# HGRN output norm per half of the columns, and splits of finished blocks queued behind the last late projection's finish

## The chip, the cores and the metric

The kernel runs on one core of a Trainium2 chip. TensorE (PE) multiplies matrices and puts its results into PSUM; VectorE (DVE), ScalarE (ACT) and GpSimd (POOL) do the elementwise work; SyncE (SP) issues most DMAs. Each engine takes its instructions from a queue of its own, in order, and waits there until the semaphores of the one at the head allow it. The metric is the device time of one launch in microseconds (us); less is better.

## The reference

One layer of a hybrid decoder trunk, in float32, on 1024 tokens of 1024 columns. A projection feeds three groups of heads, whose outputs are put side by side and multiplied by `w_out`. The change touches the norm at the end of the first group and the preparation of those outputs for `w_out`.

```python
z = rmsnorm(h, norm_mix_g[l]) @ w_in[l]
a_q, a_f, a_i, a_g, b_q, b_k, b_v, c_in = jnp.split(z, splits, axis=-1)
o_a = hgrn2_mix(a_q, a_f, a_i, a_g, lbs[l], hgrn_gnorm_g[l])
o_b = dilated_window_mix(b_q, b_k, b_v)
o_c, v_first = rwkv7_mix(c_in, ...)
h = h + jnp.concatenate([o_a, o_b, o_c], axis=-1) @ w_out[l]
...
# in hgrn2_mix, 4 heads of 128 columns, chunks of 64 tokens:
#   S_t = diag(f_t) S_(t-1) + (1 - f_t) i_t^T,  o_t = S_t^T q_t
o = o * lax.rsqrt(jnp.mean(o * o, axis=-1, keepdims=True) + NORM_EPS)
o = o.reshape(B_, S_, HG_WIDTH) * gnorm_g * jax.nn.silu(g_raw)
```

A gated MLP with a short convolution, an embedding gate and a last norm follow; they are not changed.

## The kernel before

**Products.** Each float32 operand is split into a high part, rounded to a type that PE multiplies quickly (`xh`, `whi`), and the rest (`xl`, `wlo`). A product is three matmuls: `xh` by `whi` (L137), `xl` by `whi` (L139), `xh` by `wlo` (L141). `split_x` (L157 to 162) makes the two parts of half a block of activations, 128 x 512: a cast on ACT (L160) and a subtraction (L162), on DVE for the first half of the tokens and on POOL for the second.

**The mixed stage.** Between about 440 and 600 us of the span several streams of work are interleaved. They are Python generators; `interleave` steps through them in a fixed order written out in `phase_mix` (with the tables `LATE` and `TURNS`), and the framework's scheduler then settles each engine's order from that by its own estimates. Stream A runs `hgrn_head` for heads 0 and 2, stream B for heads 1 and 3 (`handover` lets the second head of a pair begin before the first has ended). Stream C is the window attention `swa`; F is `project_late`, the projections that are left for this stage, by halves of the tokens; M is filler.

**`hgrn_head`.** For each chunk size the scores `hsc` are taken from `qt` and `ks` (L990), masked into `hS` by a predicated copy on DVE (L992), and `qt` and `hk` are scaled for the next size (L1003, L1001). Values and keys are transposed on PE (`vt`, L1018 and L1024) and copied by ACT (`hV`, L1019; `hkt`, L1025). Running states `hst` are made on DVE one from the other (L1048). The output `ho` has 1024 tokens as 8 blocks of 128, and is made in two halves of 512 columns: four blocks of matmuls into a bank of PSUM (`hpo`, L1058 and L1060) and a copy by ACT (L1061). Then comes the norm, on all 1024 columns: square on ACT (`hsq`, L1065), sums of each block on DVE (`hss`, L1067), mean and epsilon on DVE (L1068), the power -1/2 on POOL (`hrs`, L1070), the multiply on DVE (L1072). PE transposes the result, four blocks for each half (`vt`, L1078), and DVE multiplies by gain and gate (L1079). `o_split` (L1201) splits the finished block for `w_out`.

**The window attention.** PE makes logits `swq` (L1143), DVE masks them into `lg` (L1153), ACT takes the exponential (L1155), PE transposes `lg` (`swt`, L1169), ACT and DVE copy that to `pT` (L1170), PE multiplies by the values (`swo`, L1183), ACT copies to `ob` (L1184).

**PSUM.** `hsc`, `hpo`, `vt`, `swt`, `swo`, `zp` and others take turns in four banks of one pool ("mx"). PE can write a new tile only when the engine that empties the earlier tile of that bank is done.

**`project_late`.** For each left-over block of columns and each half of the tokens, 24 matmuls go into `zp`, and `finish` (L455) scales them (L320, DVE), applies a sigmoid (L460, ACT) and, for gates, multiplies (L462, DVE). The result goes to memory and is read back by the head that needs it. The last block is number 23, the gate of head 3. After it, blocks that were finished before the place for their splits existed (`self.done`: 6, 7, 0, 4, 1) are split by `o_split`, one a step. In the program's text they come behind the last projection; nothing orders them behind its `finish` in the engines' queues.

**The output projection.** `phase_out` multiplies by `w_out` (`dp`), blocks 6, 7, 0, 1, 4, 2, 3, 5 in turn. Its first matmuls fill PE from about 540 us on.

Of the kernel before, what the change touches and what calls it, by code (L numbers as in the profile page):

```python
# [10 lines left out]
F32 = mybir.dt.float32  # L11
F32R = mybir.dt.float32r
U8 = mybir.dt.uint8
AF = mybir.ActivationFunctionType
ALU = mybir.AluOpType
AX = mybir.AxisListType
PSUM = bass.MemoryType.PSUM

P = 128
T = 1024  # L20
HT = 512
# [68 lines left out]
class Trunk:  # L90
# [362 lines left out]
            yield  # L453

    def finish(self, kind, dst, src, r):  # L455
        if kind == 2:
            self.nc.vector.tensor_tensor(dst, src, r, ALU.mult)
        else:
            self.scale(src, r)
            self.nc.scalar.activation(dst, src, AF.Sigmoid)  # L460
        if kind in (1, 3):
            self.nc.vector.tensor_tensor(dst, dst, src, ALU.mult)  # L462

    def project_late(self, js):


        nc = self.nc
        for j in js:
            w = self.load_w(self.a["w_in"][j])
            t = self.keep.tile([P, T], F32, tag="zst", name=self.nm("zst"), bufs=2)  # L470
            d = self.zpool.tile([P, T], F32, tag=f"z{j}", name=f"z{j}")
            kind = (j - 8) % 4 if j < 24 else 2
            turn = j < 24 and kind < 3
            for hf in (0, 1):
                ps = self.mxp.tile([P, HT], F32, tag="mx", name=self.nm("zp"))
                self.dense({hf: ps}, w, self.X, ND, halves=(hf,))
                dst = slice((hf ^ turn) * HT, ((hf ^ turn) + 1) * HT)
                r = self.R[:, hf * HT:(hf + 1) * HT]
                self.finish(kind, t[:, dst], *((ps[:, ::-1], r[:, ::-1]) if turn and hf else (ps, r)))
                nc.sync.dma_start(d[:, dst], t[:, dst])  # L480
                if hf:
                    self.z[j] = d
                yield
        self.O = self.xall()
        for k in self.done:
            self.o_split(k)
            yield

    def zload(self, j, pool_slot, eng=None):
# [439 lines left out]
    def hgrn_head(self, h):  # L929
        nc, mxp, par, spool = self.nc, self.mxp, self.par, self.spool  # L930
        j0 = 8 + 4 * h
# [8 lines left out]
        k = self.slot("hk")  # L940
# [88 lines left out]
        def at(cc, swap=False):  # L1029
            c = (4 + cc if cc < 4 else 7 - cc) ^ (4 if swap else 0)  # L1030
            return slice(c * P, (c + 1) * P)

        for hf in (0, 1):
# [6 lines left out]
            for c in range(4):  # L1040
# [3 lines left out]
                dst = st[:, (cc + 1) * P:(cc + 2) * P]  # L1044
# [7 lines left out]
        o = self.slot("ho")  # L1052
        for hf in (0, 1):
            po = mxp.tile([P, 4, P], F32, tag="mx", name=self.nm("hpo"))
            for c in range(4):
                cc = 7 - c if hf == 0 else c
                s = at(cc)
                nc.tensor.matmul(po[:, c, :], S[:, s], V[:, s], start=True, stop=cc == 0)  # L1058
                if cc:
                    nc.tensor.matmul(po[:, c, :], qt[:, s], st[:, cc * P:(cc + 1) * P], start=False, stop=True)  # L1060
            nc.scalar.copy(o[:, hf * HT:(hf + 1) * HT], po.rearrange("p c v -> p (c v)"))  # L1061
        yield
        oa = self.zload(j0 + 3, self.slot)
        sq = self.slot("hsq")
        nc.scalar.activation(sq, o, AF.Square)  # L1065
        ss = spool.tile([P, 8], F32, tag="hss", name=self.nm("hss"))
        nc.vector.tensor_reduce(ss, sq.rearrange("p (c v) -> p c v", v=P), AX.X, ALU.add)  # L1067
        nc.vector.tensor_scalar(ss, ss, 1.0 / P, EPS, ALU.mult, ALU.add)  # L1068
        rs = spool.tile([P, 8], F32, tag="hrs", name=self.nm("hrs"))
        nc.gpsimd.tensor_tensor(rs, ss, self.mhalf[:, :8], ALU.pow)  # L1070
        o3 = o.rearrange("p (c v) -> p c v", v=P)
        nc.vector.tensor_tensor(o3, o3, rs.unsqueeze(2).broadcast_to([P, 8, P]), ALU.mult)  # L1072
        yield
        for hf in (0, 1):
            sl = slice((1 - hf) * HT, (2 - hf) * HT)
# [739 lines left out]
```

## Time and profile before

| | |
|---|---|
| median of 3 runs | 1427.42 us (1426.49 to 1429.19) |
| the profiled execution's own time | 1426.41 us |
| its span in the profile | 1424.6 us |
| mean granted clock of TensorE | 0.992 |
| four norms (square L1065, four heads) | 4.3 us of ACT |
| four norms (sums L1067 and multiply L1072) | 4.9 and 4.9 us of DVE |

In rows of a timeline the first number is the start in us from the span's start, the second the duration, then engine, line, operation, output <- input, partitions x elements, and how many such instructions stand together. What stands in brackets is the engine's idle time before the row and what ended it. In rows of groups, busy us and mean ns of one stand behind the first bar, idle time before them behind the second. A row of waits gives the waiting engine and line, the engine and line waited for, the us in total, how often, and the longest. A row of windows gives the stretch and its length, then busy us and number of instructions for PE, PE's weight loads, DVE, ACT and POOL, the granted clock of PE, the DMA share and GB/s.

### The profile page before, as it was taken

The page shows a single profiled execution, that of the slowest core. Times are in us where ns is not written, and L with a number is a line of the kernel's source. Part 1 is how long each engine was busy: PE and PEld are TensorE (multiplying, and loading weights), DVE is VectorE, ACT ScalarE, POOL GpSimd, SP SyncE. Part 2 cuts the span into 40 slices and gives each one's busy share as a digit, 9 for nine tenths or more (in the row PEclk, how much of TensorE's full clock was granted, in tenths as well). Part 3 has the DMA queues.
Part 4 walks back from the last instruction along what each step waited for, and adds up shares of the span by engine and source line. Part 5 has one row for each costly group of instructions (what it writes and reads, how often), then busy time and mean ns, then how long its engine had stood idle before and what let it go on. Part 6 is the DMA issues. An engine that isn't in the chain of part 4 may idle for free.

```text
span 1424.6 us, 22342 instructions
## 1 busy us (share of the span) xinstructions
PE 1381.9 (97%) x8642; PEld 1118.0 (78%) x8642; DVE 1066.8 (75%) x1629; ACT 602.5 (42%) x1015; POOL 392.5 (28%) x286
## 2 busy tenths in 40 slices
PE   8989999999999999999999999999999999999996
PEld 6768777777778768787788888888888888888885
DVE  7597363964666796468788888898888799778675
ACT  7411323123155485254544444443434444455542
POOL 5321012210122141221244544454543000002431
PEclk9999999999999999999999999999999999999998
DMA  6124111240432211753332233333324963441443
GB/s 220 45 82 119 61 46 61 81 119 32 154 143 104 84 61 40 262 178 117 119 111 91 94 106 102 106 102 111 112 96 147 356 214 111 126 141 47 135 158 113
DMA packets 80122, 167.61 MB, mean 118 GB/s; under 512 B 19984, under 2 KB 22288, under 8 KB 80016
## 3 DMA queue, kind: packets, MB, share of 16 engines
q1 hardware_dynamic: 66496, 146.52, 30.6%
q10 hardware_dynamic: 12656, 16.52, 3.4%
q0 software_dynamic: 864, 3.15, 0.6%
q8 instruction: 68, 1.11, 0.3%
q14 instruction: 38, 0.31, 0.1%
HBM read 119.76 MB, written 46.40 MB: 117 GB/s over the span
## 4 chain that ended last, share of the span: by engine, by line
PE 48%; issue 3%; DVE 2%; POOL 1%; ACT 1%; DMA 0%; POOLq 0%; ACTq 0%; DVEq 0%
PE bg L1302 16%; PE bv L1302 12%; PE bv L1596 7%; PE bg L1596 7%; PE dp L141 1%; PE dp L137 1%; PE dp L139 1%; POOL wlo L116 1%; PE bv L137 0%; PE bv L139 0%; PE bv L141 0%; DVE h L1692 0%; POOL xh L162 0%; DVE gt L1691 0%; ACT whi L114 0%
## 5 line engine op out<-in xcount | busy, mean ns | idle before, releaser
L137 PE MATMUL dp<-xh,whi 128*128 128x512 f32 x544 | 189.2, 408 | 6.9 <-DVE r L501 2.9
L139 PE MATMUL dp<-xl,whi 128*128 128x512 f32 x544 | 182.7, 396 | 0.8 <-DVE xl L411 0.8
L141 PE MATMUL dp<-xh,wlo 128*128 128x512 f32 x544 | 181.1, 394 | 0.0
L116 POOL TENSOR_TENSOR wlo<-wraw,whi 128x512 fp32r<-128x512 f32 x60 | 81.6, 1360 | 321.4 <-ACT whi L114 257.1
L116 POOL TENSOR_TENSOR wlo<-raw,whi 128x512 fp32r<-128x512 f32 x84 | 134.7, 1622 | 76.0 <-ACT whi L114 76.0
L114 ACT CAST whi<-wraw 128x512 fp32r<-128x512 f32 x120 | 72.8, 617 | 155.7 <-PE dp L139 107.3
L1302 PE MATMUL bg<-t,whi 128*128 128x512 f32 x352 | 133.3, 389 | 0.0
L137 PEld LDWEIGHTS dp<-xh,whi 128*128 128x128 f32 x544 | 99.4, 189 | 34.9 <-issue 6.2
L139 PEld LDWEIGHTS dp<-xl,whi 128*128 128x128 f32 x544 | 102.2, 189 | 23.8 <-DVE xl L411 1.1
L141 PEld LDWEIGHTS dp<-xh,wlo 128*128 128x128 f32 x544 | 102.7, 189 | 22.9 <-issue 0.8
L116 POOL TENSOR_TENSOR wlo<-s,whi 128x512 fp32r<-128x512 f32 x44 | 64.0, 1454 | 175.0 <-ACT whi L114 175.0
L1596 PE MATMUL bg<-t,whi 128*128 128x512 f32 x308 | 95.3, 390 | 0.0
L1596 PE MATMUL bv<-t,whi 128*128 128x512 f32 x308 | 94.8, 389 | 0.0
L114 ACT CAST whi<-raw 128x512 fp32r<-128x512 f32 x88 | 52.6, 619 | 94.3 <-issue 48.3
L114 ACT CAST whi<-s 128x512 fp32r<-128x512 f32 x66 | 38.9, 620 | 121.4 <-PE bg L1302 113.6
L1302 PEld LDWEIGHTS bg<-t,whi 128*128 128x128 f32 x352 | 66.1, 188 | 13.6
L190 POOL TENSOR_TENSOR rst<-rst,mhalf 128x4 f32<-128x4 f32 (+1 forms) x9 | 9.9, 1102 | 235.6 <-DVE rst L186 218.5
L1302 PE MATMUL bg<-t,wlo 128*128 128x512 f32 x176 | 67.2, 389 | 0.0
L1596 PEld LDWEIGHTS bv<-t,whi 128*128 128x128 f32 x308 | 57.9, 188 | 11.9
L1596 PEld LDWEIGHTS bg<-t,whi 128*128 128x128 f32 x308 | 57.8, 188 | 12.0
L1592 ACT CAST t<-t 128x512 fp32r<-128x512 f32 x77 | 47.8, 622 | 45.5 <-PE bv L1596 31.8
L116 DVE TENSOR_TENSOR wlo<-wraw,whi 128x512 fp32r<-128x512 f32 x60 | 49.7, 829 | 20.6 <-ACT whi L114 20.4
(417 smaller groups left out, 3415.1 us busy)
## 6 DMA issues: line engine op xcount, KB each, us to landing
raw<-in_ffn_up_dram SPq DMA_DIRECT2D x44, 512.0 KB, 3.5
wraw<-in_w_in_dram SPq DMA_DIRECT2D x28, 512.0 KB, 3.4
z<-zst SPq DMA_DIRECT2D x18, 512.0 KB, 2.8
gb<-ct SPq DMA_DIRECT2D x33, 256.0 KB, 2.2
t<-gb SPq DMA_DIRECT2D x33, 256.0 KB, 2.7
t<-gt SPq DMA_DIRECT2D x33, 256.0 KB, 2.7
zl<-z SPq DMA_DIRECT2D x16, 512.0 KB, 4.2
wraw<-in_ple_gate_dram SPq DMA_DIRECT2D x16, 512.0 KB, 3.4
```

The source lines that it names most:

```text
L114: self.cast = nc.scalar.copy(hi, src).ins
L116: eng.tensor_tensor(lo, src, hi.bitcast(F32), ALU.subtract)
L137: nc.tensor.matmul(ps[hf], wh, xh[hf], start=first, stop=False)
L139: nc.tensor.matmul(ps[hf], wh, xl[hf], start=False, stop=False)
L141: nc.tensor.matmul(ps[hf], wl, xh[hf], start=False, stop=last)
L190: nc.gpsimd.tensor_tensor(r2, r, self.mhalf[:, :n], ALU.pow)
L1302: nc.tensor.matmul(ps, w[part == 2][:, s], X[k][part == 1], start=start and k == part == 0, stop=k == 3 and part == 2, skip_group_check=no ...
L1592: nc.scalar.copy(xh, x)
L1596: nc.tensor.matmul(ps[m], wt[part == 2][:, m * P:(m + 1) * P], (xh, xl)[part == 1], start=k == part == 0, stop=k == NK - 1 and part == 2)
```

## The change

`finish` returns the instructions that end it. `project_late` keeps those of its last call, the second half of block 23 (a sigmoid on ACT and a multiply on DVE), and issues each of the five waiting `o_split` behind them (`issue_after`): 10 casts on ACT, 5 subtractions on DVE and 5 on POOL. This sets an order in the queues; it adds no data dependence and no DMA.

In `hgrn_head` square and sums are taken per half, each right behind the copy of that half; the gate's load and the tiles of the norm are taken before the first copy; the multiply is written as two of 512 columns. Mean and power stay as they were, one instruction each for both halves. No matmul is added or taken away.

```diff
--- before.py
+++ after.py
@@ -453,13 +453,15 @@
             yield
 
     def finish(self, kind, dst, src, r):
+        ends = []
         if kind == 2:
-            self.nc.vector.tensor_tensor(dst, src, r, ALU.mult)
+            ends.append(self.nc.vector.tensor_tensor(dst, src, r, ALU.mult))
         else:
             self.scale(src, r)
-            self.nc.scalar.activation(dst, src, AF.Sigmoid)
+            ends.append(self.nc.scalar.activation(dst, src, AF.Sigmoid))
         if kind in (1, 3):
-            self.nc.vector.tensor_tensor(dst, dst, src, ALU.mult)
+            ends.append(self.nc.vector.tensor_tensor(dst, dst, src, ALU.mult))
+        return ends
 
     def project_late(self, js):
 
@@ -476,14 +478,17 @@
                 self.dense({hf: ps}, w, self.X, ND, halves=(hf,))
                 dst = slice((hf ^ turn) * HT, ((hf ^ turn) + 1) * HT)
                 r = self.R[:, hf * HT:(hf + 1) * HT]
-                self.finish(kind, t[:, dst], *((ps[:, ::-1], r[:, ::-1]) if turn and hf else (ps, r)))
+                ends = self.finish(kind, t[:, dst], *((ps[:, ::-1], r[:, ::-1]) if turn and hf else (ps, r)))
                 nc.sync.dma_start(d[:, dst], t[:, dst])
                 if hf:
                     self.z[j] = d
                 yield
         self.O = self.xall()
         for k in self.done:
-            self.o_split(k)
+            with ExitStack() as order:
+                for i in ends:
+                    order.enter_context(self.tc.issue_after(i.ins))
+                self.o_split(k)
             yield
 
     def zload(self, j, pool_slot, eng=None):
@@ -1058,18 +1063,21 @@
                 nc.tensor.matmul(po[:, c, :], S[:, s], V[:, s], start=True, stop=cc == 0)
                 if cc:
                     nc.tensor.matmul(po[:, c, :], qt[:, s], st[:, cc * P:(cc + 1) * P], start=False, stop=True)
-            nc.scalar.copy(o[:, hf * HT:(hf + 1) * HT], po.rearrange("p c v -> p (c v)"))
-        yield
-        oa = self.zload(j0 + 3, self.slot)
-        sq = self.slot("hsq")
-        nc.scalar.activation(sq, o, AF.Square)
-        ss = spool.tile([P, 8], F32, tag="hss", name=self.nm("hss"))
-        nc.vector.tensor_reduce(ss, sq.rearrange("p (c v) -> p c v", v=P), AX.X, ALU.add)
+            s = slice(hf * HT, (hf + 1) * HT)
+            if hf == 0:
+                oa = self.zload(j0 + 3, self.slot)
+                sq = self.slot("hsq")
+                ss = spool.tile([P, 8], F32, tag="hss", name=self.nm("hss"))
+            nc.scalar.copy(o[:, s], po.rearrange("p c v -> p (c v)"))
+            nc.scalar.activation(sq[:, s], o[:, s], AF.Square)
+            nc.vector.tensor_reduce(ss[:, 4 * hf:4 * hf + 4], sq[:, s].rearrange("p (c v) -> p c v", v=P), AX.X, ALU.add)
+        yield
         nc.vector.tensor_scalar(ss, ss, 1.0 / P, EPS, ALU.mult, ALU.add)
         rs = spool.tile([P, 8], F32, tag="hrs", name=self.nm("hrs"))
         nc.gpsimd.tensor_tensor(rs, ss, self.mhalf[:, :8], ALU.pow)
         o3 = o.rearrange("p (c v) -> p c v", v=P)
-        nc.vector.tensor_tensor(o3, o3, rs.unsqueeze(2).broadcast_to([P, 8, P]), ALU.mult)
+        for c in (slice(0, 4), slice(4, 8)):
+            nc.vector.tensor_tensor(o3[:, c], o3[:, c], rs[:, c].unsqueeze(2).broadcast_to([P, 4, P]), ALU.mult)
         yield
         for hf in (0, 1):
             sl = slice((1 - hf) * HT, (2 - hf) * HT)
```

The first place is DVE's queue at the norm of head 0, beside a `pT` copy of the window attention (`hss` sums, `ho` output, `hrs` power; `hS` and `qt` are another head's masked scores and queries). Before:

```order
L1067 TENSOR_REDUCE hss_745_4528<-hsq_744_4526 128x8
L1170 COPY pT_734_4494<-swt_736_4501 128x384
L1170 COPY pT_737_4506<-swt_739_4513 128x384
L1068 TENSOR_SCALAR hss_745_4528<-hss_745_4528 128x8
L992 COPY_PREDICATED hS_683_4210<-cmask_77,hsc_747_4534 128x4x64
L1072 TENSOR_TENSOR ho_724_4433<-ho_724_4433,hrs_746_4531 128x1024
L1003 TENSOR_TENSOR qt_671_4148<-qt_671_4148,hT_684_4212 128x2x32x8
```

After the change:

```order
L1073 TENSOR_REDUCE hss_728_4446<-hsq_727_4445 128x4
L997 COPY_PREDICATED hS_683_4210<-cmask_77,hsc_730_4461 128x4x64
L1008 TENSOR_TENSOR qt_671_4148<-qt_671_4148,hT_684_4212 128x2x64x4
L1073 TENSOR_REDUCE hss_728_4446<-hsq_727_4445 128x4
L1075 TENSOR_SCALAR hss_728_4446<-hss_728_4446 128x8
L1080 TENSOR_TENSOR ho_724_4433<-ho_724_4433,hrs_746_4533 128x512
L1178 COPY pT_737_4502<-swt_739_4509 128x384
L1178 COPY pT_740_4514<-swt_742_4521 128x384
L1080 TENSOR_TENSOR ho_724_4433<-ho_724_4433,hrs_746_4533 128x512
L997 COPY_PREDICATED hS_683_4210<-cmask_77,hsc_747_4537 128x4x64
L1008 TENSOR_TENSOR qt_671_4148<-qt_671_4148,hT_684_4212 128x2x32x8
```

The sums stand in two rows, the scaling (now L1075) and the first half of the multiply have moved ahead of both `pT` copies, and the second half stands behind them.

The second place is ACT's queue at the end of the last late projection, from the casts ahead of the sigmoid on (`whi` is a cast of weights). Before:

```order
L160 CAST xh_885_5252<-zl_827_4970 128x512
L114 CAST whi_1017_5897<-wraw_1015_5895 128x512
L160 CAST xh_891_5258<-ob_635_3976 128x512
L160 CAST xh_895_5262<-oc_295_1813 128x512
L114 CAST whi_1020_5901<-wraw_1015_5895 128x512
L160 CAST xh_897_5264<-oc_546_3441 128x512
L460 ACT_TABLE_LOAD
L460 ACTIVATE zst_838_4990<-zp_874_5180 128x512
L1019 COPY hV_875_5209<-vt_876_5210 128x512
L1019 COPY hV_875_5209<-vt_877_5216 128x512
L1025 COPY hkt_878_5222<-vt_879_5223 128x512
L1025 COPY hkt_878_5222<-vt_880_5229 128x512
```

After the change:

```order
L114 CAST whi_1020_5913<-wraw_1015_5907 128x512
L461 ACT_TABLE_LOAD
L461 ACTIVATE zst_838_4996<-zp_874_5186 128x512
L1024 COPY hV_875_5215<-vt_876_5216 128x512
L1024 COPY hV_875_5215<-vt_877_5222 128x512
L160 CAST xh_911_5284<-oc_295_1813 128x512
L160 CAST xh_895_5268<-oc_295_1813 128x512
L160 CAST xh_913_5286<-oc_546_3441 128x512
L1030 COPY hkt_878_5228<-vt_879_5229 128x512
L1030 COPY hkt_878_5228<-vt_880_5235 128x512
L160 CAST xh_897_5270<-oc_546_3441 128x512
L1192 COPY ob_822_4951<-swo_919_5304 128x128
```

The casts `xh` have left the place ahead of the sigmoid; three of them stand between the `hV` and the `hkt` copies now and others further down, between the copies of the window attention.

The third place is DVE's queue at the norm of head 2. Before:

```order
L1067 TENSOR_REDUCE hss_950_5464<-hsq_949_5462 128x8
L992 COPY_PREDICATED hS_870_5156<-cmask_77,hsc_952_5470 128x4x64
L1068 TENSOR_SCALAR hss_950_5464<-hss_950_5464 128x8
L1003 TENSOR_TENSOR qt_855_5086<-qt_855_5086,hT_871_5158 128x2x32x8
L1072 TENSOR_TENSOR ho_943_5421<-ho_943_5421,hrs_951_5467 128x1024
L1170 COPY pT_959_5515<-swt_961_5522 128x384
L1170 COPY pT_962_5527<-swt_964_5534 128x384
```

After the change:

```order
L1073 TENSOR_REDUCE hss_947_5440<-hsq_946_5439 128x4
L997 COPY_PREDICATED hS_870_5162<-cmask_77,hsc_949_5455 128x4x64
L1008 TENSOR_TENSOR qt_855_5092<-qt_855_5092,hT_871_5164 128x2x64x4
L1073 TENSOR_REDUCE hss_947_5440<-hsq_946_5439 128x4
L1013 TENSOR_TENSOR hT_871_5164<-hT_871_5164 128x16
L162 TENSOR_TENSOR xl_910_5283<-ob_822_4951,xh_909_5282 128x512
L1075 TENSOR_SCALAR hss_947_5440<-hss_947_5440 128x8
L997 COPY_PREDICATED hS_870_5162<-cmask_77,hsc_952_5479 128x4x64
L1080 TENSOR_TENSOR ho_943_5427<-ho_943_5427,hrs_951_5475 128x512 x2
L1008 TENSOR_TENSOR qt_855_5092<-qt_855_5092,hT_871_5164 128x2x32x8
L1178 COPY pT_959_5524<-swt_961_5531 128x384
L1178 COPY pT_962_5536<-swt_964_5543 128x384
```

A moved subtraction (`xl_910`) stands between the second sum and the scaling, and both halves of the multiply and a `qt` stand ahead of the `pT` copies.

On PE, at the norm of head 3, the transposes `vt` of the normed output stand among matmuls of the output projection. Before:

```order
L139 MATMUL dp_1014_5846<-xl_904_5271,whi_1002_5828 128x512
L139 MATMUL dp_1014_5846<-xl_888_5255,whi_1002_5828 128x512
L141 MATMUL dp_1014_5846<-xh_903_5270,wlo_1003_5830 128x512
L141 MATMUL dp_1014_5846<-xh_887_5254,wlo_1003_5830 128x512
L137 MATMUL dp_1022_5910<-xh_911_5278,whi_1012_5842 128x512
L1078 MATMUL vt_998_5758<-cst_76,ho_991_5728 128x128 x4
L1078 MATMUL vt_999_5764<-cst_76,ho_991_5728 128x128 x4
L137 MATMUL dp_1022_5910<-xh_895_5262,whi_1012_5842 128x512
```

After the change:

```order
L139 MATMUL dp_1014_5858<-xl_904_5277,whi_1002_5840 128x512
L139 MATMUL dp_1014_5858<-xl_888_5261,whi_1002_5840 128x512
L1086 MATMUL vt_998_5770<-cst_76,ho_991_5737 128x128 x4
L1086 MATMUL vt_999_5776<-cst_76,ho_991_5737 128x128 x4
L141 MATMUL dp_1014_5858<-xh_903_5276,wlo_1003_5842 128x512
L141 MATMUL dp_1014_5858<-xh_887_5260,wlo_1003_5842 128x512
L137 MATMUL dp_1022_5922<-xh_911_5284,whi_1012_5854 128x512
L137 MATMUL dp_1022_5922<-xh_895_5268,whi_1012_5854 128x512
```

The eight transposes stand three output matmuls earlier.

## The prediction

> **What bounds the kernel now.** I read the views in this order: the page's busy times, for the engine that sets the time; the table of windows, for the stretch in which the changed instructions run; PE's waits in that stretch, as the most that can be won there; then the timeline around each wait.
>
> ```profile
> span 1424.6 us, 22342 instructions
> ...
> PE 1381.9 (97%) x8642; PEld 1118.0 (78%) x8642; DVE 1066.8 (75%) x1629; ACT 602.5 (42%) x1015; POOL 392.5 (28%) x286
> ```
> ```profile
> 440.00:600.00 160.00, 152.45 (x1368) 123.59 (x1365) 113.61 (x226) 82.15 (x160) 44.83 (x36) 1.00 0.33 116
> 580.00:620.00 40.00, 40.00 (x178) 33.14 (x177) 17.24 (x25) 12.29 (x21) 9.16 (x7) 1.00 0.63 224
> ```
> ```profile
> PE vt L1078 <- DVE ho L1072: 3.0, 2, 1.8
> PE vt L1024 <- ACT hV L1019: 2.4, 1, 2.4
> PE hsc L990 <- DVE qt L1003: 1.0, 2, 0.6
> PE zp L137 <- DVE pT L1170: 0.5, 1, 0.5
> PE swt L1169 <- DVE hS L992: 0.2, 1, 0.2
> PE zp L137 <- ACT hV L1019: 0.2, 1, 0.2
> ```
>
> TensorE (PE) is busy 97% of the span, and the change takes no matmul away. Every changed instruction runs between 440 and 600 us, where PE is idle for 160.00 - 152.45 = 7.55 us at full granted clock (the 1.00 behind POOL's column). The six waits make 7.3 of that. So 7.3 us, 0.51% of the time, is the most that the change can win. It can lose more, because VectorE (DVE) has 113.61 busy us of these 160 and stands in most of those rows. From 580 on PE has no idle time at all. A shift of PE's work at 575 thus reaches the end one for one, and the sum below is a sum of PE's waits.
>
> **The prices.** The norm is now done on 512 columns.
>
> ```profile
> L215 ACT ACTIVATE sqt<-h 128x512 f32<-128x512 f32 x41 | 25.6, 631 | 46.4 <-DVE h L1692 20.7 <-DVE h L1232 15.9 <-DVE acc L216 3.9
> L1065 ACT ACTIVATE hsq<-ho 128x1024 f32<-128x1024 f32 x4 | 4.3, 1068 | 0.1
> L1067 DVE TENSOR_REDUCE hss<-hsq 128x8 f32<-128x1024 f32 x4 | 4.9, 1218 | 5.1 <-ACT hsq L1065 5.1
> L1072 DVE TENSOR_TENSOR ho<-ho,hrs 128x1024 f32<-128x1024 f32 x4 | 4.9, 1226 | 6.2 <-POOL hrs L1070 6.2
> ```
>
> A half square costs 0.63 us (the 128x512 square of L215), so two cost 0.19 more than one whole. No row shows a half reduce or half multiply. Each lies between half of the whole, 0.61, and the whole, 1.22. I take 0.61, since the square at half size comes near half. Twenty-four such halves replace twelve wholes, and ACT and DVE have 49% and 29% of the stretch idle, so their added work costs PE something only where it stands ahead of something that PE waits for. The small scaling (TENSOR_SCALAR) and the power on POOL still take both halves at once. A tile's power therefore starts after its second reduce, 0.63 - 1.07 + 0.61 - 1.22 = about 1.05 us sooner at best, and the first half of the multiply ends 0.61 sooner again.
>
> [...]
>
> **Head 0 (456 to 465 us).**
>
> ```profile
> 456.50 1.05 ACT L1065 ACTIVATE hsq<-ho 128x1024 f32<-128x1024 f32 x1
> ...
> 456.67 1.27 POOL L1001 TENSOR_TENSOR hk<-hk,hT 128x512 f32<-128x512 f32 x1 [5.62 <-ACT ks L977]
> ...
> 458.72 1.01 DVE L1170 COPY pT<-swt 128x384 f32<-128x384 f32 x2
> ...
> 459.36 1.71 PE L1183 MATMUL swo<-pT,sV 128*64 128x128 f32 x28
> ...
> 459.89 1.67 POOL L1070 TENSOR_TENSOR hrs<-hss,mhalf 128x8 f32<-128x8 f32 x1 [1.96 <-DVE hss L1068]
> ...
> 463.56 0.69 PE L990 MATMUL hsc<-qt,ks 128*64 128x64 f32 x16 [0.59 <-DVE qt L1003]
> ...
> 464.80 0.50 PE L137 MATMUL zp<-xh,whi 128*128 128x512 f32 x1 [0.55 <-DVE pT L1170]
> ```
>
> Before, DVE made its two pT copies at 458.72, ahead of the scaling and the multiply, and PE entered swo at 459.36, whose bank of PSUM the first copy empties. Now the scaling and the first half multiply stand ahead of both copies. Second half square 456.50 to 457.13; half reduce to 457.8; POOL free of hk at 457.94; the power until about 459.6; half multiply until 460.3; the first copy (half of 1.01) until 460.8. PE waits 460.8 - 459.36 = 1.4. That delay swallows the later waits of 0.59 and 0.55, for qt and pT, which DVE reaches before PE now. Net 1.4 - 1.14 = **+0.3**. Bounds: -1.1, if the copies are hardly late; +0.6 with a power of 2.01 (its longest, below).
>
> **Head 1 (500 to 507 us).**
>
> ```profile
> 500.04 2.01 POOL L1070 TENSOR_TENSOR hrs<-hss,mhalf 128x8 f32<-128x8 f32 x1 [6.42 <-DVE hss L1068]
> ...
> 504.55 0.69 DVE L320 TENSOR_TENSOR zp<-zp,rstd 128x512 f32<-128x512 f32 x1
> ...
> 505.64 0.55 PE L1169 MATMUL swt<-cst,lg 128*128 128x128 f32 x3 [0.16 <-DVE hS L992]
> ```
>
> Nothing on PE waited for this multiply. After it, the scaling of the projection's first half, which was done at 504.55, now stands behind the hk, zl and qt rows of head 2, some 2 us later, and the mask copy and qt for the second-last scores behind that. I work out 0.45 us of wait for that qt in place of the 0.16. **+0.3**, bounds -0.2 (the wait goes) and +1.2 (the 2 us less 0.8, which four window matmuls that now run ahead fill: half of the eight's 1.56 in the next view).
>
> **The late projection's end (519 to 540 us).** This is the moved split. Ten ACT casts, five DVE and five POOL subtractions now stand behind the finish's sigmoid and multiply; no DMA and no matmul are issued by them.
>
> ```profile
> 519.33 1.77 DVE L162 TENSOR_TENSOR xl<-zl,xh 128x512 fp32r<-128x512 f32 x1
> ...
> 520.50 1.72 POOL L162 TENSOR_TENSOR xl<-ob,xh 128x512 fp32r<-128x512 f32 x1
> ...
> 520.56 1.56 PE L1143 MATMUL swq<-zl,zl 64*128 64x512 f32 x8
> ...
> 522.68 0.69 DVE L320 TENSOR_TENSOR zp<-zp,rstd 128x512 f32<-128x512 f32 x1
> ...
> 524.53 0.66 PE L1024 MATMUL vt<-cst,hk 128*128 128x128 f32 x4 [2.41 <-ACT hV L1019]
> ...
> 535.49 0.62 ACT L160 CAST xh<-ob 128x512 fp32r<-128x512 f32 x1 [1.03 <-DVE ob L1194]
> ...
> 536.49 0.69 DVE L162 TENSOR_TENSOR xl<-ob,xh 128x512 fp32r<-128x512 f32 x1
> ...
> 536.60 1.76 PE L1169 MATMUL swt<-cst,lg 128*128 128x128 f32 x12
> ...
> 537.09 0.34 DVE L1048 SCALAR_TENSOR_TENSOR hst<-hst,hT,hkv 128x128 f32<-128x128 f32 x1
> ```
>
> Before, the scaling at 522.68 stood behind long subtractions on DVE, the sigmoid behind it, and ACT's hV copies behind the sigmoid; PE waited 2.41 for a bank of PSUM that hV empties. With the splits behind, scaling and sigmoid end earlier and hV is ready when PE gets there: -2.4. But the ten splits now run where ACT and DVE carry head 2. Taking each cast at 0.62 and each subtraction at 0.69: three casts between hV and hkt make a window transpose wait 0.2; a DVE subtraction ahead of the mask copy, 0.55; a pT copy behind it ahead of the state, 0.2; the chain of state updates (hst), with the moved work between its links, ends at 537.1 to 537.7 where PE, about 0.7 ahead of its 536.60 of before, comes at 535.9 to the window transposes whose copies stand behind it, 1.2; four casts ahead of ob and pT on ACT, 0.6. That is 2.7. Net **+0.3**, bounds -2.4 (none of them bites) and +1.7 (they make 4.1, with hst at its late end and the pT copy at 1.0).
>
> **Head 2 (544 to 557 us).**
>
> ```profile
> 547.79 1.23 DVE L1072 TENSOR_TENSOR ho<-ho,hrs 128x1024 f32<-128x1024 f32 x1 [1.53 <-POOL hrs L1070]
> ...
> 549.16 1.06 PE L1078 MATMUL vt<-cst,ho 128*128 128x128 f32 x8 [1.18 <-DVE ho L1072]
> ...
> 556.90 0.69 PE L990 MATMUL hsc<-qt,ks 128*64 128x64 f32 x16 [0.43 <-DVE qt L1003]
> ```
>
> One moved subtraction (0.69) stands between the second reduce and the scaling, and eats most of the 1.05 won. The first four transposes then wait 0.4 instead of 1.18. The second four write into a bank that a pT copy empties, and that copy stands behind both half multiplies and a qt now: 1.2. Two later score groups wait 0.15 and 1.0 for their qt, against 0.43. Net 2.75 - 1.61 = about 1.1, of which some 0.3 is the same lateness counted twice: **+0.8**, bounds -1.2 (the 1.18 goes, nothing comes) and +2.0 (the whole multiply late as well).
>
> **Head 3 (568 to 575 us).**
>
> ```profile
> 568.77 1.06 ACT L1065 ACTIVATE hsq<-ho 128x1024 f32<-128x1024 f32 x1
> ...
> 571.78 0.62 PE L141 MATMUL dp<-xh,wlo 128*128 128x512 f32 x2
> ...
> 572.24 0.39 PE L137 MATMUL dp<-xh,whi 128*128 128x512 f32 x1
> ...
> 574.42 1.06 PE L1078 MATMUL vt<-cst,ho 128*128 128x128 f32 x8 [1.79 <-DVE ho L1072]
> ```
>
> Here the chain stands free: 574.42 - 568.77 = 5.65 us from square to transpose. It loses a half reduce and a half multiply, 1.22 (the two half squares run after the second copy, so nothing is won there). But PE's transposes now stand three output matmuls earlier, and wait from that earlier place: 0.7 us, by the 572.24 - 571.78 = 0.46 for two of them. Wait 1.79 - 1.22 + 0.7 = 1.3. **-0.5**, bounds -1.2 (the place costs nothing) and 0.
>
> **The sum**: 0.3 + 0.3 + 0.3 + 0.8 - 0.5 = +1.2 us on the profiled execution's 1426.41 (its span of 1424.6 and 1.8 around it), 1427.6. That execution lies 1.01 below the median of the runs shown, 1427.42; with it, 1427.42 + 1.2 = **1428.6**.
>
> **The rivals.** *A, waits go and none come.* The finish is no longer held up, and the added instructions fall into idle time: for it speaks that the 2.41 is the largest wait and that its cause, casts and subtractions ahead of a finish, is removed for certain. Terms: late projection -2.4, head 2 -1.2, head 3 -0.5, heads 0 and 1 nothing: -4.1, **1423.3**. Against it: DVE is 71% busy here, and its queue is what the moved work joins.
>
> *B, slower: POOL's subtractions meet DVE's.* The rows at 519.33 and 536.49 have the same subtraction at 1.77 us beside POOL's at 520.50, and at 0.69 alone. Five moved POOL subtractions now run from 524 to 545, beside DVE's hk, qt and subtraction rows of head 2, all with two operands in SBUF. If three on the way to hst, some 1.0 longer each, fall under them, the late projection's term becomes +3.3 and the sum +4.2: **1431.6**. It decides from the point where the state chain ends past 537.7. Against it: POOL's share here is only 44.83 of 160. [...]
>
> *C, the halves shorten nothing.* In heads 1 and 3 the order has both half reduces next to each other, behind both copies, and the power needs both. Then only the late projection's +0.3 remains: **1427.7**.
>
> **How the numbers follow.** The forecast has a chance of 0.44, C 0.14, A 0.24, B 0.18. A measurement of this kernel tells about 0.2% (2.85 us) from no change: 1424.6 to 1430.3 counts as the same. A lies below it, B above, the forecast and C inside: faster 0.24, same 0.58, slower 0.18. The range goes from A to B, 1423.2 to 1431.8; what lies outside is a case with still other bounds reached together. The forecast's own cases lie between 1426 and 1430.3.
>
> **What would show it.** In the profile of the changed kernel: no wait of vt for hV, and the scaling within 2 us of the projection's last matmul; a wait of swo for pT of 1 to 1.5 near 459; waits of the window transposes on DVE between 526 and 537, with subtractions of 1.7 there under B and 0.7 under the forecast; vt of head 2 waiting twice, on ho and on pT; vt of head 3 waiting about 1.3. PE's idle time between 440 and 600 should be about 8.8 us. It is wrong if that is below 6 (A) or above 11 (B), or if time moves outside the stretch, where no instruction is changed.

## The result, and the profile after

| | before | changed |
|---|---|---|
| median, 10 runs each | 1428.24 us (1425.96 to 1429.41) | 1431.86 us (1428.95 to 1435.46) |
| changed over before, 95% interval | | 1.0025 [1.0014, 1.0037] |
| profiled execution | 1426.41 us | 1432.13 us |

The change costs 3.6 us by the medians, 2.0 to 5.3 by the interval. 1428.6 was forecast and the range ended at 1431.8: the direction was right, and both the size and the range fell short.

Three views of the changed kernel: the page's span and busy times, the window of 440 to 600 us, and the sums of PE's waits from 440 to 606 us, the stretch that the change touches.

```profile
span 1430.4 us, 22353 instructions
...
PE 1386.5 (97%) x8642; PEld 1119.6 (78%) x8642; DVE 1066.1 (75%) x1637; ACT 603.4 (42%) x1019; POOL 393.2 (27%) x286
```
```profile
440.00:600.00 160.00, 150.72 (x1391) 121.86 (x1390) 113.50 (x234) 83.82 (x166) 43.17 (x35) 1.00 0.32 111
```
```profile
PE vt L1086 <- DVE ho L1080: 1.6, 1, 1.6
PE swt L1177 <- DVE hst L1053: 1.5, 1, 1.5
PE swo L1191 <- DVE pT L1178: 1.5, 1, 1.5
PE hsc L995 <- DVE qt L1008: 1.3, 3, 0.6
PE hkv L1044 <- DVE pT L1178: 1.1, 1, 1.1
PE vt L1086 <- DVE pT L1178: 1.0, 1, 1.0
PE vt L1086 <- ACT pT L1178: 0.4, 1, 0.4
PE swt L1177 <- DVE hS L997: 0.4, 1, 0.4
```

PE's idle time in the stretch went from 7.55 to 160.00 - 150.72 = 9.28 us. The wait of 2.4 for `hV`, the largest before, is gone, and five new ones have come: `swo` for `pT`, `swt` for `hst`, `hkv` for `pT`, and the two `vt` of head 2 for `pT` (1.0 for DVE's copy, 0.4 for ACT's).

**How much of it is the stretch's.** The two profiled spans differ by 5.8 us, more than the medians. So the experiments are read by one number, the **shift of the stretch**: the time from the first `hpo` near 452 us to one later addition of the output projection, compared with before (worked out from starts in nanoseconds, so that the last digit can differ from that of the rows). First before, then the changed kernel, rows of the timeline:

```profile
451.80 0.38 PE L1058 MATMUL hpo<-hV,hS 128*128 128x128 f32 x2
...
617.07 0.68 DVE L1232 TENSOR_TENSOR h<-h,dp 128x512 f32<-128x512 f32 x1
```
```profile
454.71 0.38 PE L1063 MATMUL hpo<-hV,hS 128*128 128x128 f32 x2
...
622.81 0.68 DVE L1240 TENSOR_TENSOR h<-h,dp 128x512 f32<-128x512 f32 x1
```

The stretch takes 168.10 us in the changed kernel and 165.27 before, so its shift is **2.83**. The other 2.9 us were lost ahead of it, where the instructions are the same and PE's waits are no longer (17.4 us in all up to 450 us before, 16.7 changed). The window of 90 to 100 us shows what differs there, first before, then changed:

```profile
90.00:100.00 10.00, 7.93 (x33) 5.59 (x32) 8.28 (x16) 3.27 (x5) 1.28 (x1) 1.00 0.49 127
```
```profile
90.00:100.00 10.00, 7.92 (x26) 5.47 (x25) 8.46 (x16) 3.27 (x5) 1.28 (x1) 0.83 0.50 127
```

The mean granted clock there is 0.83 against 1.00. The trace has 3.4 us of half clock in that window (0.50 from 96.2 to 99.4 us). The rows of ACT and DVE that lay 0.15 to 0.19 us earlier than in before ahead of it lie 1.38 later from 200 us on, so this dip cost about 1.55 us. The changed profile has a second such dip near 362 (0.50 from 362.6 to 365.8 us). Other runs have them at other times (near 551 us in e1, near 525 in e9), so a single time, or a single span, is uncertain by one or two steps of about 1.5 us, and the shift of the stretch is not, unless a dip falls into it (two runs below).

### The profile page after: what moved, and what is told of

The parts are those of the page before. It is cut to its first block, busy times and chain, and to the rows that moved or that the text cites. A ratio compares the mean times of both kernels' runs of the same rounds, so it can differ in the third digit from the quotient of the medians.

```text
span 1430.4 us, 22353 instructions
## 1 busy us (share of the span) xinstructions
PE 1386.5 (97%) x8642; PEld 1119.6 (78%) x8642; DVE 1066.1 (75%) x1637; ACT 603.4 (42%) x1019; POOL 393.2 (27%) x286
## 4 chain that ended last, share of the span: by engine, by line
PE 48%; issue 3%; DVE 2%; POOL 1%; ACT 1%; DMA 0%; POOLq 0%; ACTq 0%; DVEq 0%
PE bg L1310 16%; PE bv L1310 12%; PE bv L1604 7%; PE bg L1604 7%; PE dp L141 1%; PE dp L137 1%; PE dp L139 1%; POOL wlo L116 1%; PE bv L137 0%; PE bv L139 0%; PE bv L141 0%; DVE h L1700 0%; POOL xh L162 0%; ACT whi L114 0%; DVE gt L1699 0%
```

## The experiments

All shifts are against the profile of before. Each shift comes from one profile. Ratios are of medians, to the kernel before on the same chip.

| run | shift, us | ratio, 95% interval |
|---|---|---|
| changed kernel | 2.83 | 1.0025 [1.0014, 1.0037] |
| e1 splits only | 3.31 (a dip inside) | 1.0014 [1.0005, 1.0024] |
| e2 halves only | 2.27 | 1.0023 [1.0007, 1.0039] |
| e3 changed, POOL only writes | 0.97 | 1.0009 [0.9995, 1.0023] |
| e4 changed, splits on DVE | 1.25 | one run, no ratio |
| e5 before, block 1 behind the finish | -0.80 | 0.9988 [0.9976, 1.0] |
| e6 before, blocks 4 and 1 behind it | 0.06 | 1.0006 [0.9991, 1.002] |
| e7 before, splits on DVE | -0.83 | 0.9986 [0.9977, 0.9996] |
| e8 splits behind the finish on DVE, head 3 halved | -0.82 | 0.9987 [0.9975, 0.9998] |
| e9 before, head 0 halved | 0.40 (a dip inside) | one run, no ratio |
| e10 before, head 1 halved | 1.26 | one run, no ratio |
| e11 e7 with head 3 halved | -0.98 | 0.9993 [0.9982, 1.0004] |
| e12 e11 with block 1 behind the finish | -0.66 | 0.9992 [0.998, 1.0004] |

### e1 and e2: one part each

e1 is before with the first three hunks of the diff (`finish`, `project_late`); e2 is before with the last two (`hgrn_head`).

> Only the five splits are queued behind the last late projection's finish; the norm is the one of before. The number looked at beside the time is the shift of PE's work over the stretch: how much later than in the profile of before the output projection's matmuls at 580 us run, less how much later hpo at 450 us runs (the changed kernel: 5.75 - 2.91 = 2.85 us). Theory S (the moved splits cost most): shift +1.5 to +2.5, the wait of vt for hV (2.41) gone, waits of hkv for pT (about 1.1) and of a window transpose for hst (about 1.5) as in the changed kernel, time about +0.15% (2 us). Theory H (the halved norm costs most): shift below +0.7, time the same.

> Only the norm by halves; the splits are placed as before. Theory S: shift of the stretch between -0.5 and +0.7 (head 0 +0.4, head 1 +0.3, heads 2 and 3 together -0.2 to -1.2), the wait of vt for hV still there, time the same as before within 0.1%. Theory H: shift +1.5 or more, time about +0.15%.

PE's waits of e1, then of e2:

```profile
PE vt L1083 <- DVE ho L1077: 4.1, 2, 2.3
PE swt L1174 <- DVE hst L1053: 1.5, 1, 1.5
PE hkv L1044 <- DVE pT L1175: 1.1, 1, 1.1
```
```profile
PE vt L1081 <- DVE ho L1075: 3.3, 2, 1.7
PE swt L1172 <- DVE hS L992: 1.7, 1, 1.7
PE swo L1186 <- DVE pT L1173: 1.5, 1, 1.5
PE swo L1186 <- DVE zst L462: 0.7, 1, 0.7
PE vt L1024 <- ACT hV L1019: 0.4, 1, 0.4
```

e1 has the changed kernel's waits for `hst` and `pT` within 0.01, as theory S has it. Its shift of 3.31 holds a clock dip of 3.4 us at 551 us (mean granted clock 0.83 from 545 to 555 us); less what such a dip cost near 96 us (1.55) or in e9 below (0.85) it is 1.8 to 2.5, and the ratio says 2.0. e2 goes against theory S: the halves alone cost 2.27, which is what theory H asked for, and the wait for `hV` falls to 0.4 though no split is ordered behind the finish. So each part costs about two, and together they cost 2.83, less than the sum. "The splits or the halves" was the wrong question: both lay out the queues of PE, DVE and ACT anew between 505 and 530 us. What of the loss they share was not separated.

### e3 and e4: is it POOL?

The changed profile shows DVE rows of very different length for the same operation. Its timeline, DVE, POOL and PE around the two largest new waits:

```profile
529.55 1.27 POOL L162 TENSOR_TENSOR xl<-oc,xh 128x512 fp32r<-128x512 f32 x1 [2.65 <-ACT xh L160]
530.03 1.34 DVE L162 TENSOR_TENSOR xl<-oc,xh 128x512 fp32r<-128x512 f32 x1 [0.34 <-ACT xh L160]
...
531.57 1.27 POOL L162 TENSOR_TENSOR xl<-oc,xh 128x512 fp32r<-128x512 f32 x1 [0.74 <-ACT xh L160]
531.62 1.76 DVE L1008 TENSOR_TENSOR qt<-qt,zl 128x512 f32<-128x512 f32 x1
533.31 0.28 DVE L1178 COPY pT<-swt 128x128 f32<-128x128 f32 x1
...
540.27 1.32 POOL L162 TENSOR_TENSOR xl<-ob,xh 128x512 fp32r<-128x512 f32 x1
540.65 1.50 DVE L162 TENSOR_TENSOR xl<-zl,xh 128x512 fp32r<-128x512 f32 x1
542.07 0.34 DVE L1053 SCALAR_TENSOR_TENSOR hst<-hst,hT,hkv 128x128 f32<-128x128 f32 x1
...
542.46 0.87 PE L1177 MATMUL swt<-cst,lg 128*128 128x128 f32 x6 [1.52 <-DVE hst L1053]
```

Each of the three long DVE rows runs beside a moved POOL subtraction. The `qt` of 1.76 stands directly ahead of the `pT` copy that `hkv` waits for (1.10), and the subtraction of 1.50 directly ahead of the last `hst`.

```diff
# e3, in o_split (src stands for self.o[k][:, hf * HT:(hf + 1) * HT])
-            self.split_x(self.O[k], hf, src, alt=hf)
+            if hf and k in self.done:
+                nc.scalar.copy(self.O[k][0][hf], src)
+                nc.gpsimd.memset(self.O[k][1][hf].bitcast(F32), 0.0)
+            else:
+                self.split_x(self.O[k], hf, src, alt=hf)
# e4, in o_split
-            self.split_x(self.O[k], hf, src, alt=hf)
+            self.split_x(self.O[k], hf, src, alt=hf and k not in self.done)
```

> The changed kernel, with POOL's five moved subtractions replaced by writing zeros (the low parts of the second half of five blocks are left out); the order on PE, DVE and ACT is that of the changed kernel. Theory C (POOL's moved subtractions lengthen DVE's two-input instructions on the way to hkv and hst): the subtraction rows of 1.34 and 1.50 and the qt row of 1.76 on DVE fall to about 0.69, hkv's wait for pT from 1.10 to below 0.3, the window transpose's wait for hst from 1.52 to below 0.9, shift of the stretch from 2.85 to about 1.0, time about 1.9 us less than the changed kernel. Rival Q (the place in DVE's and ACT's queues alone costs it): those waits stay within 0.3 of the changed kernel and the shift stays above 2.4.

> The changed kernel, with all ten moved subtractions on DVE and none on POOL. Theory C: DVE's subtraction and qt rows between the finish and hst are all at 0.7 or below, the wait for hst is below 1.5 although DVE has five rows more, shift 1.5 to 3. Rival Q: the five added rows of 0.69 come on top, the waits for pT and hst grow to 2 or more each, shift 4 or more.

The same rows in e3:

```profile
528.52 0.69 DVE L162 TENSOR_TENSOR xl<-oc,xh 128x512 fp32r<-128x512 f32 x1 [0.35 <-ACT xh L160]
...
529.46 0.69 DVE L1008 TENSOR_TENSOR qt<-qt,zl 128x512 f32<-128x512 f32 x1
530.06 0.28 DVE L1178 COPY pT<-swt 128x128 f32<-128x128 f32 x1
...
537.76 0.68 DVE L162 TENSOR_TENSOR xl<-zl,xh 128x512 fp32r<-128x512 f32 x1
...
538.75 0.66 PE L1177 MATMUL swt<-cst,lg 128*128 128x128 f32 x4 [1.06 <-DVE hst L1053]
...
539.86 0.44 PE L1177 MATMUL swt<-cst,lg 128*128 128x128 f32 x2 [0.45 <-ACT ob L1192]
```

The three DVE rows are at 0.68 to 0.69, and the order of instructions on PE, DVE and ACT in the stretch is that of the changed kernel. The wait of `hkv` is gone and the shift fell from 2.83 to 0.97, as theory C had it (1.0). The wait for `hst` is 1.06 (below 0.9 was expected), and a wait of 0.45 for ACT's `ob` follows right behind it: together they are as long as the 1.52 of the changed kernel, so at this place nothing was won. The zeros were written at 520 to 524 us, 0.53 each, since they wait for no cast; so e3 shows what POOL's subtractions cost by being there at all, and not which part of a POOL instruction does it. e4 has no such shortcut: all ten subtractions stand on DVE, five rows more than in the changed kernel, and still the shift is 1.25, less than half of the changed kernel's. Its `qt` is at 0.69 and its three first subtractions together at 1.90. The shift lies below the 1.5 to 3 that theory C gave, and other waits came: 0.65 of `hkv` for ACT's `pT` and 1.35 of the window transposes for ACT's `ob`. Rival Q asked for 4 or more; this decides against it.

### e5, e6, e7 and e8: less of it moved, or none

```diff
# e5: splits only, and of those block 1 (e6: blocks 4 and 1)
-                for i in ends:
+                for i in ends if k in (1,) else ():
# e7: before with e4's line
# e8: splits only with e4's line, and in hgrn_head the halves for h == 3 alone
```

> The norm of before, and of the five splits only that of block 1 queued behind the finish; the other four where they were. Theory: few moved instructions join the queues that carry head 2, so the new waits for pT and hst (1.10 and 1.51 with all five moved) stay below 0.5 each, but casts and subtractions of blocks 6 and 7 still stand ahead of the finish, so the wait of vt for hV goes from 2.41 to between 1 and 2. Shift of the stretch -1.2 to +0.3, time the same. Rival (any moved split costs what five do): shift +1 or more.

> The norm of before, and the splits of blocks 4 and 1 queued behind the finish. As with block 1 alone, between that and all five: wait of vt for hV 0.5 to 2, waits for pT and hst together 0.5 to 1.5; shift -1 to +1, time the same. Rival: shift +1 or more.

> Before, with nothing moved and the norm whole, but all ten early subtractions on DVE and none on POOL. Theory C: DVE's rows of 1.67, 1.77 and 1.75 ahead of the finish fall to 0.69 each, so that five more rows of 0.69 fit in their time; the finish's scaling starts at 520.5 to 522 of that profile's time and the wait of vt for hV falls from 2.41 to 0.5 to 1.8: shift -0.6 to -2, time 0.05 to 0.15% less. Rival Q (rows in the queue cost, not POOL): scaling later than 522.7, wait 2.4 or more, shift 0 to +2.

> All five splits behind the finish with all ten subtractions on DVE (as e4), and the norm by halves for head 3 only. Against e4 (shift 1.25) the wait of swo for pT near 460 (1.50) turns into the two of before (0.59 and 0.55) and that for qt near 508 (0.60) goes: shift about +0.4 (-0.4 to +1.0), time the same as before. If the halves of heads 0 to 2 were worth something, it is above 1.25.

DVE ahead of the finish in before, then in e7:

```profile
517.73 1.67 DVE L162 TENSOR_TENSOR xl<-oc,xh 128x512 fp32r<-128x512 f32 x1
519.33 1.77 DVE L162 TENSOR_TENSOR xl<-zl,xh 128x512 fp32r<-128x512 f32 x1
521.02 1.75 DVE L116 TENSOR_TENSOR wlo<-wraw,whi 128x512 fp32r<-128x512 f32 x1
```
```profile
520.50 1.35 DVE L162 TENSOR_TENSOR xl<-oc,xh 128x512 fp32r<-128x512 f32 x1
...
521.89 0.63 DVE L162 TENSOR_TENSOR xl<-oc,xh 128x512 fp32r<-128x512 f32 x1
522.45 1.28 DVE L162 TENSOR_TENSOR xl<-zl,xh 128x512 fp32r<-128x512 f32 x2
523.65 0.68 DVE L162 TENSOR_TENSOR xl<-ob,xh 128x512 fp32r<-128x512 f32 x1
524.25 0.68 DVE L162 TENSOR_TENSOR xl<-zl,xh 128x512 fp32r<-128x512 f32 x1
524.86 0.68 DVE L320 TENSOR_TENSOR zp<-zp,rstd 128x512 f32<-128x512 f32 x1
```

The time axis of e7 lies 4.16 us later at the first `hpo` (dips ahead of it), so its scaling at 524.86 answers to 520.70 in before, where it started at 522.68. The first subtraction still takes 1.35, beside a multiply of POOL (`hk`, from 519.67, 1.62 long). The five behind it take the time of two of before, and no wait comes in place of what is won: PE's wait for `hV` is 1.3 against 2.4, the others are those of before. e7 was a forecast of theory C on the kernel before, and it came out inside it (-0.83 in -0.6 to -2). e5 wins as much (-0.80) in another way, with the waits for `hV` at 0.78 (1 to 2 was expected) and for `hst` at 0.26. With blocks 4 and 1 (e6) the wait for `hst` is 1.19, that of head 2's `vt` 1.50 in place of e5's 1.12, and all is given back (0.06). Between e4 and e8 the norms of heads 0 to 2 are whole again, and the shift goes from 1.25 to -0.82: their halves cost 2.1 there. e8 was expected at -0.4 to +1.0, so the halves cost more than was thought.

### e9 and e10: which head's halves

> Before, with the norm by halves for head 0 only; PE's order is that of before. Theory: the wait of swo for pT (1.50) takes the place of the two of 0.59 and 0.55, nothing else changes: shift +0.4 (0.3 to 0.5). Rival (the change near 460 us comes from another edit): no wait of swo, shift 0.

> Before, with the norm by halves for head 1 only. Theory: PE never waits for head 1's norm, so its halves win nothing, but DVE's and ACT's queues are laid out anew behind it, with subtractions and head 2's first rows ahead of the late finish: the waits of swo for zst (0.69) and of the window transpose for hS (1.69), as with all heads halved, shift +1.0 to +2.0. Rival (what the halves of heads 2 and 3 add makes those waits): shift below +0.6.

DVE at head 0 in the changed kernel, then in e9:

```profile
462.73 0.69 DVE L1080 TENSOR_TENSOR ho<-ho,hrs 128x512 f32<-128x512 f32 x1 [1.77 <-POOL hrs L1077]
463.34 1.01 DVE L1178 COPY pT<-swt 128x384 f32<-128x384 f32 x2
```
```profile
461.05 0.69 DVE L1082 TENSOR_TENSOR ho<-ho,hrs 128x512 f32<-128x512 f32 x1 [1.08 <-POOL hrs L1079]
461.66 0.55 DVE L1180 COPY pT<-swt 128x384 f32<-128x384 f32 x1
```

e9's 0.40 agrees with the expectation by accident. In e9 the scheduler left one `pT` copy ahead of the first half multiply. PE's wait for `pT` is 0.42, not 1.50, and takes the place of two that made 1.14. By 474 us the stretch had gained 0.45; the rest is a clock dip at 525 (mean granted clock 0.83 from 520 to 530 us). So the halves at head 0 can win, and what costs in the changed kernel is that the first half multiply stands ahead of **both** copies, where DVE waits 1.77 for POOL's power.

e10 came out as expected (1.26; waits of `swo` for `zst` 0.69 and of `swt` for `hS` 1.69). PE waits for no result of head 1's norm, yet halving it alone costs 1.26: its five rows in place of three change the scheduler's layout of all that follows up to 530 us. The wait for `hV` fell to 0.38 in e10, and more than that was lost behind it.

### e11 and e12: can the gains be put together

> As e7 (nothing moved, the ten early subtractions on DVE), and the norm by halves for head 3 only. e7's shift of -0.83 and what head 3's shorter chain gives (1.79 to 1.60 in the wait of vt, -0.2): shift -1.0 (-0.7 to -1.4), time 0.1 to 0.2% less than before. Rival (halves cost at every head): shift above -0.7.

> As e11, and block 1's split queued behind the finish as in e5. If the gains of e5 and e7 were of different waits they would add up: shift -1.8 to -2.2. I expect that they are the same wait (of PE for hV, 2.41 in before, 0.78 in e5, 1.32 in e7), so that at most what is left of it goes: shift -1.0 to -1.6, time 0.1 to 0.2% less.

e11's shift is -0.98: head 3's halves add 0.15 to e7, as expected. In time it can't be told from no change (0.9993). In e12 the gains do not add up; the wait of head 2's `vt` grew to 1.51 and the shift is -0.66, short of what was expected. By time e5, e7 and e8 lie below both kernels, with ratios to before of 0.9986 to 0.9988 that can't be told apart; the interval of e7 (1425.59 us, [0.9977, 0.9996]) stays furthest from no change, that of e5 reaches 1.0.

## Why the prediction was wrong

Term by term, from the starts on PE of the first transposes behind head 0 (470.40 and 473.72), of `hpo` of head 2 (538.20 and 543.32), of `hkv` of head 3 (562.19 and 568.38) and the row at 617 us, each less what the shift was before it; the same for e3:

| term | forecast | changed | e3, without POOL's subtractions |
|---|---|---|---|
| head 0 | +0.3 | +0.41 | +0.41 |
| head 1 and the late projection's end | +0.6 | +1.80 | +0.54 |
| head 2 | +0.8 | +1.07 | +0.44 |
| head 3 | -0.5 | -0.45 | -0.42 |
| sum | +1.2 | +2.83 | +0.97 |

The windows from the first `hpo` to the row at 617 us show what these sums are made of, in before, the changed kernel and e3:

```profile
451.80:617.07 165.27, 157.72 (x1360) 128.67 (x1359) 111.76 (x212) 82.76 (x159) 45.14 (x35) 1.00 0.36 123
```
```profile
454.71:622.81 168.10, 158.82 (x1360) 128.96 (x1359) 111.09 (x220) 83.28 (x163) 44.89 (x35) 1.00 0.34 118
```
```profile
453.09:619.33 166.24, 158.90 (x1360) 128.91 (x1359) 108.18 (x219) 83.05 (x163) 41.15 (x35) 1.00 0.34 120
```

PE's idle time (length less busy time) is 7.55, 9.28 and 7.34 us. Its busy time for the same 1360 matmuls, whose ends the profile models, is 157.72, 158.82 and 158.90.

- **The step that failed** is the one that began "Taking each cast at 0.62 and each subtraction at 0.69". The waits that came were named correctly, but DVE's rows were priced alone. `qt` took 1.76 where 0.69 was assumed and `xl` 1.50, and `hkv` waits 1.10 in place of 0.2. With the same order in the queues but without POOL's subtractions (e3) PE is idle for 1.94 us less and the shift is 1.86 less, which is more than the 1.63 by which the sum fell short. The wait for `hst`, 1.52 in place of 1.2, is not part of this: e3 loses 1.51 there, to `hst` and `ob`.
- **A second step failed with it**: "the sum below is a sum of PE's waits". Of the 2.83 only 1.73 is idle time (1.2 was forecast); the other 1.10 is longer busy time for the same matmuls, which the prediction put at nothing. e3 and e4 have it too (1.18 and 1.15), e2, with the halves alone, has none (157.71).
- **That e3 comes near the forecast 1.2 is luck.** Without POOL's subtractions PE is idle for 0.21 us less than before, where the forecast had 1.2 more; the longer busy time makes up the rest. In the row of the late projection's end PE's waits sum to 2.72 before, 3.80 changed and 2.27 in e3. The places in the queues were priced too high, and what POOL does to DVE's rows was left out.
- **Rival B was the case that happened**, at two thirds of its price (+2.83 against +4.2); its sign of more than 11 us of idle time did not show (9.28). It had a chance of 0.18, on the ground that POOL is busy for only 44.83 of 160 us. That was the wrong measure. The moved subtractions become ready together, behind one finish, when DVE does its two-input work on the same blocks; the mean share says nothing of that. The profile of before had the evidence in the rows of 1.67 to 1.77 just ahead of the finish.
- **Head 0** was right in mechanism and size: `swo` waits 1.50 (1.4 forecast). **Head 3** was right in mechanism, but its wait fell from 1.79 to 1.60 (1.3 forecast), by 0.2 and not 0.5. The -0.45 in the table comes near by luck: one matmul that was counted there before now falls into head 2's row. The half sum and half multiply each take 0.69, not the 0.61 taken.
- **Head 2** was right in part: the second `vt` waits 0.95 for `pT` (1.2 forecast). The first waits 0.43 where 0.4 was forecast, but for a `pT` copy on ACT and not for `ho`, which is luck; in e3 this wait is gone. The two later score groups wait 0.26 and 0.46 where 0.15 and 1.0 were forecast.
- **Rival A** fell, since the wait for `hV` did go, but new ones came. **Rival C** fell by e2: the halves change the layout and cost 2.27.
- **The range** took B's sum as its upper end and left nothing for the scatter of the medians; the median of before itself was 1427.42 in three runs and is 1428.24 in ten.

What stays open is where the 1.10 us of busy time come from. PE's matmuls in the stretch are the same, but some stand in smaller groups, with a few more changes between kinds; that this is the cause was not tried. Nor is it settled whether the 0.8 us between the shift and the medians is more than scatter; the interval holds 2.83.

## What to carry to other kernels

Before elementwise work is moved, look at what the neighbouring engine does at the new place, and price each two-input DVE instruction twice, alone and beside a POOL instruction, from rows of both kinds in the profile of before (here `xl` took 0.69 us alone and 1.77 beside POOL's); two such instructions on DVE alone (1.28 us) were cheaper here than one on each engine side by side (1.67 to 1.77). An edit that shortens a chain nobody waits for can still cost, when a scheduler lays out the queues behind it anew: compare the order before the time. Measure a change of a few us by the shift between two rows around it, since whole executions differ by clock dips.

## What the runs showed of the hardware that was not expected

The profiles of this kernel's versions differ by steps: stretches of 3.4 us, and one of 6.8, in which the granted clock is 0.50. Between 30 and 1400 us the profile of before has one, from 663.6 us, and that of the changed kernel three, from 96.2, 362.4 and 669.6 us; the one of 6.8 is in before, from 8.2 us. The one near 96 in the changed kernel moved what follows by about 1.55 us. It begins 1.5 us behind the end of a wait of PE of 2.07 us, and the one near 362 at the end of a wait of 2.38. In e1 and e9 the first PE row behind a wait of 2.29 and of 2.41 us is the slowed one. Not every such wait has a dip at it: before has the waits of 2.07 and 2.38 too, ending at 94.82 and 361.00 us, and both kernels have one of 1.94 to 1.95, ending at 705.43 and 711.22, and the granted clock behind all four is 1.00. Timeline rows of PE in the changed kernel, in e9, and last in before:

```profile
94.63 1.10 PE L636 MATMUL bon<-bv,cst 128*128 128x512 f32 x2 [2.07 <-DVE bv L628]
```
```profile
525.31 1.12 PE L1024 MATMUL vt<-cst,hk 128*128 128x128 f32 x4 [2.41 <-ACT hV L1019]
```
```profile
524.53 0.66 PE L1024 MATMUL vt<-cst,hk 128*128 128x128 f32 x4 [2.41 <-ACT hV L1019]
```

The last row has the wait of the second, 2.41, and its four transposes take 0.66 us; in e9 the same four take 1.12. The same wait thus came with a dip in one execution and without one in the other. The dip in e9 cost 0.85 us (the shift of 0.40 and the 0.45 gained by 474 us). What sets the length of 3.4 us was not shown. That the dips hang on such waits was not tried by an experiment here, and near 664 us, where the waits are 0.56 and 0.76, it does not fit.
